# Padding the large tiles of a hybrid RG-LRU, attention and expert-choice block to 256-byte offsets, and other forms for its routing

## The chip, the cores and the metric

The kernel runs on one core of a Trainium2 chip. The metric is device time in microseconds of one execution. The kernel before takes 1211.78 us (median of 3 runs, 1211.24 to 1212.25).

## The reference, cut to what matters

One transformer-like block over 1024 tokens of width 1024, all in float32: a modulated norm, an input projection into five parts, a recurrent branch (a short convolution and two gated linear recurrences), a differential attention branch with 4 heads, an output projection, and a feed-forward part in which each of 16 experts chooses its 128 tokens.

```python
h = rms_norm(x, g_norm1) * (1.0 + scale1) + shift1
x_lru, z_lru, q, k, v = jnp.split(jnp.dot(h, w_in), SPLITS, axis=-1)
y_lru = (rg_lru(conv(x_lru), forward) + rg_lru(conv(x_lru), backward)) * gelu(z_lru)
y_att = diff_attention(q, k, v, ...)
x = x + gate1 * jnp.dot(concat([y_lru, y_att]), w_out)
h2 = rms_norm(x, g_norm2) * (1.0 + scale2) + shift2
aff = softmax(jnp.dot(h2, w_router))              # [1024, 16]
g, idx = top_k(aff.T, 128)                        # 128 tokens for each expert
xe = h2[idx]
y = (silu(xe @ w1[e]) * (xe @ w3[e])) @ w2[e] * g # for e in 16 experts, 1024 x 1024 each
x = x + gate2 * scatter_add(idx, y)
```

## The kernel before, in words

A float32 value is split into two float32r parts, hi (a copy, ScalarE) and lo (the rest, a subtraction on VectorE or GpSimd), and a product takes three matmuls: hi by hi, hi by lo, lo by hi. All of these go through the helper at L92; their tiles tell them apart. A matmul here has 512 columns of a moving operand against a 128x128 stationary operand, which a weight load brings in for each matmul.

The stages in order: the input stage with the first projections (tiles `pjx`, moving operand `hh`/`hl` of pool `hp`, stationary `w0h`/`w0l` of pool `ylp`); projections `pjq`, `pjk`, `pjz`, `pjv` (operands in pools `hp` and `strm`), with the recurrences beside them; attention (`sc`, `pw`, `pv`); the output projection `mix` in eight token tiles t, with the norm, the router's logits and their softmax for each t; the routing; and the experts.

The mix stage (L1010 to L1101) runs, for each t: split the activations (`yh`, `yl`, pool `xw`), 48 matmuls against `who`/`wlo`/`wos` (pools `wo1` and `qkp`), add `x` (L1027), square sums on ScalarE, an inverse square root by three Newton steps on VectorE (L1054 to L1062, operands of one column), the logits (`pl`, `pk`), the softmax (L1072 to L1078, in the SBUF tile `lg`), values below the smallest normal number set to zero and each of 16 columns repeated 8 times (`afd`, L1081), a copy to `affs` (L1083), a transpose `pq` and two copies of it, `aTh` (the upper halves, as bfloat16) and `aT`, which have 128 rows (expert e, digit j) and 1024 tokens. The last tile, t = 7, is cut in three column pieces (`mix`, `mix7b`, `mix7c`).

The routing (L1169 to L1220) finds each expert's 128th largest value by nine counts. A count (L1124 to L1131) compares 1024 tokens with a threshold per row on VectorE (`junk`, with the sum in `cnt`), turns the sum into 0 or 1 (`sat`), and adds the 8 digits of an expert by a matmul with `bone`; then the next threshold `thr` and its companion `cth` are made (L1134, L1180, and `stp` at L1182). The operands are one to seven columns wide. Meanwhile GpSimd splits `affs` in three bfloat16 parts (L1145 to L1149) and makes `wl` of the first three weight tiles. The chosen slots, the pick of indices for expert 0, its gather and some filler matmuls (`warm`) follow.

The experts: 24 weight tiles each (16 of w1 and w3, 8 of w2; 512 KB each), which the SP queue loads into a ring of 37 buffers from several pools; a load is issued when the buffer's last tile has been split. Each tile is split into `wh` (ScalarE, 3 buffers) and `wl` (VectorE, 3 buffers), both in pool `wo1`, and used as moving operand in 6 matmuls: 96 of `ab` (stationary `xeh`, `xel`, pool `moe`), then 48 of `y` (stationary `hth`, `htl`, pool `moe`). The tokens of the next expert are picked meanwhile: GpSimd makes the one-hot tiles `oh` (8 instructions, L1236), which start when the transposes `pf` have freed their buffer; 8 small matmuls `pi`, queued on TensorE between `y` of this expert and `ab` of the next, read them; a gather by GpSimd follows.

SBUF is laid out by pools: some stack up from the low end (`const`, `ylp`, `qkp` or `lru`, `wo1`, `late0`, `late`, `moe`), others down from the high end (`rawA`, `vp`, `hp`, `strm`, later `ap`, `xw`). Tiles begin at multiples of 32 bytes. With the sizes of the small tiles as they are, the start addresses modulo 256 are: 96 in `ylp`, `qkp`, `lru`, `wo1`, `late0` and `late`; 160 in `moe`; 224 in `rawA`, `vp`, `hp`, `strm` and the large tiles of `xw`; 32 in `ap`. A large tile has 4096 bytes per partition, and its parts used by one matmul are multiples of 512 bytes apart, so all matmuls of a kind have the same two residues.

The order of instructions on VectorE and TensorE is as written in the routing; in the mix stage and the experts a planner sets it, with `issue_after` as the only hints.

Of the kernel before, what the change touches and what calls it, by code (L numbers as in the profile page):

```python
# [18 lines left out]
P = 128  # L19
# [6 lines left out]
NE = 16  # L26
# [55 lines left out]
def tile_block(ctx: ExitStack, tc, x, cols, w_mod, b_mod, w_in, wa, wx, lam_qk, relT, w_out, g2, w_router,  # L82
# [17 lines left out]
    SY.dma_start(out=col, in_=cols)  # L100
    epsc = const.tile([P, 1], F32, name="epsc")
    V.memset(epsc, EPS)

# [7 lines left out]


    rawA = ctx.enter_context(tc.tile_pool(name="rawA", bufs=NRA, side="right"))
    vp = ctx.enter_context(tc.tile_pool(name="vp", bufs=1, side="right"))
# [66 lines left out]
    gqk = tbl.tile([P, 2], F32, name="gqk")  # L181
    go8 = const.tile([P, 1], F32, name="go8")
    jb = const.tile([P, 1], I32, name="jb")
    jf = const.tile([P, 7], F32, name="jf")
    relt = tbl.tile([NH, 32], F32, name="relt")
    A.dma_start(out=relt, in_=relT)
    nlam = const.tile([P, 1], F32, name="nlam")
    ls = const.tile([P, 2], F32, name="ls")
    lq = sm1.tile([P, 4, 64], F32, name="lq")
# [505 lines left out]
    s_sum = const.tile([P, NH, NT, 2], F32, name="s_sum")  # L695
    stat0 = const.tile([P, 1, 3], F32, name="stat0")
    scp, pt_, wts, pvs, ots = {}, {}, {}, {}, {}
# [85 lines left out]
    phw = ExitStack()  # L783
    psa = phw.enter_context(tc.tile_pool(name="psa", bufs=1, space=PSUM, reuse_waits="tile"))
    stat = ap.tile([P, NH * NT - 1, 3], F32, name="stat")

# [111 lines left out]
    with tc.manual_schedule(engines={mybir.EngineType.PE, mybir.EngineType.DVE, mybir.EngineType.Activation}):  # L898
        for g in range(NG + 2):
# [54 lines left out]
    xt_ = {nm: xw.tile(sh, F32, name=nm) for nm, sh in (  # L954
        ("sum4", [P, NE]), ("wr2", [P, KT, NE]), ("wrA", [P, KT, 32]), ("lg", [P, NT, NE]), ("hov", [P, 4]), ("hot", [P, 4]),
        ("hoy", [P, 4]), ("l4", [P, P]), ("afd", [P, P]))}
    xb_ = {nm: xw.tile([P, D], F32R if nm[0] == "y" else F32, tag=nm, bufs=1, name=nm + "_0") for nm in XO}
# [24 lines left out]
    rs2 = const.tile([P, NT], F32, name="rs2")  # L982
    lg = xt_["lg"]
    lmx = const.tile([P, 2 * NT], F32, name="lmx")
    aT = late0.tile([P, S], F32, tag="big", bufs=1, name="aT")
    lsc = late.tile([P, S], F32, tag="big", bufs=1, name="lsc")
    aTh = lsc[:, 0:512].bitcast(BF16)
    rstm = lsc[:, 512:640].bitcast(BF16).rearrange("p (a t) -> p a t", t=NT)
    rem = lsc[:, 640:768].rearrange("p (t e) -> p t e", e=NE)
# [16 lines left out]
    for t in range(NT):  # L1006
# [46 lines left out]
        if t == NT - 1:  # L1053
            V.tensor_tensor(out=ssq2[:, t, 0:1], in0=ssq2[:, t, 0:1], in1=ssq2[:, t, 1:2], op=ALU.add)  # L1054
        v, u, y = ssq2[:, t, 0:1], ssq2[:, t, len(cuts) - 2:len(cuts) - 1], rs2[:, t:t + 1]
        V.scalar_tensor_tensor(out=v, in0=v, scalar=EPS, in1=u, op0=ALU.add, op1=ALU.add)
        V.tensor_scalar(out=y.bitcast(I32), in0=v.bitcast(I32), scalar1=1, scalar2=None, op0=ALU.logical_shift_right)
        V.tensor_scalar(out=v, in0=v, scalar1=-0.5, scalar2=None, op0=ALU.mult)
        V.tensor_scalar(out=y.bitcast(I32), in0=y.bitcast(I32), scalar1=-1, scalar2=0x5F3759DF, op0=ALU.mult, op1=ALU.add)
        for _ in range(3):  # L1060
            V.scalar_tensor_tensor(out=u, in0=y, scalar=v, in1=y, op0=ALU.mult, op1=ALU.mult)
            V.scalar_tensor_tensor(out=y, in0=u, scalar=1.5, in1=y, op0=ALU.add, op1=ALU.mult)  # L1062
        pl = psa.tile([P, P], F32, tag="pv", bufs=1, name=f"pl{t}")
        for k in range(KT):
# [5 lines left out]
        mm(pl[:, 0:NE], l4, sum4, True, True)  # L1070
        lt = lg[:, t, :]
        V.scalar_tensor_tensor(out=lt, in0=pl[:, 0:NE], scalar=rs2[:, t:t + 1], in1=s2w, op0=ALU.mult, op1=ALU.add)  # L1072
# [4 lines left out]
        V.reciprocal(out=sm, in_=sm)  # L1077
        V.tensor_scalar(out=lt, in0=lt, scalar1=sm, scalar2=None, op0=ALU.mult)  # L1078
        afd = xt_["afd"]
        ltb = lt.unsqueeze(2).to_broadcast([P, NE, 8])  # L1080
        i_afd = V.scalar_tensor_tensor(out=afd.rearrange("p (e j) -> p e j", j=8), in0=ltb, scalar=TINY, in1=ltb,  # L1081
                                       op0=ALU.is_ge, op1=ALU.mult)
        i_aff = V.tensor_copy(affs[:, t, :], afd.rearrange("p (e j) -> p e j", j=8)[:, :, 0])  # L1083
        pq = psa.tile([P, P], F32, tag="pv", bufs=1, name=f"pq{t}")
        T.transpose(pq, afd, ident)
        act(aTh[:, sl], pq.bitcast(BF16)[:, 1::2])
        i_aT = act(aT[:, sl], pq)
        (A if t in OA else SY).dma_start(out=out[sl, :], in_=x1)
        if t < NT - 1:
# [21 lines left out]
    junk = moe.tile([P, S], BF16, tag="os", bufs=1, name="junk")  # L1111
    lo = const.tile([P, 1], I32, name="lo")
    thr = const.tile([P, 1], I32, name="thr")
    ni = const.tile([P, 1], I32, name="ni")
    cnt = const.tile([P, 1], F32, name="cnt")
    sat = const.tile([P, 1], BF16, name="sat")
    cth = const.tile([P, 1], F32, name="cth")
    pw8 = const.tile([P, 7], F32, name="pw8")
    stp = const.tile([P, 7], F32, name="stp")
    lof, thf = lo.bitcast(F32), thr.bitcast(F32)  # L1120
    for i in range(7):
        G_.memset(pw8[:, i:i + 1], 2.0 ** (-5 - 3 * i))

    def count(name, src, during=()):  # L1124
        first = V.tensor_scalar(out=junk, in0=src, scalar1=thf, scalar2=None, op0=ALU.is_ge, op1=ALU.add, accum_out=cnt)
        V.tensor_scalar(out=sat, in0=cnt, scalar1=float(CAP), scalar2=None, op0=ALU.is_ge)
        for f_ in during:
            f_()
        pn = pst.tile([P, 1], F32, tag="pn", bufs=2, name=name)
        mm(pn, bone, sat, True, True)  # L1130
        return pn, first  # L1131

    def axpy(o, a, b, c):
        return lambda: V.scalar_tensor_tensor(out=o, in0=a, scalar=b, in1=c, op0=ALU.mult, op1=ALU.add)  # L1134

    NR = 5
    rhs = late.tile([P, NT, NE, NR], BF16, name="rhs")
    tidx = late.tile([P, NT], F32, name="tidx")
    pidx = late.tile([P, 1], F32, name="pidx")
# [11 lines left out]
    G_.tensor_copy(selb, bone.rearrange("p (e j) -> p e j", j=8)[:, :, 0])  # L1151
    sts = const.tile([P, 1], F32, name="sts")
    idx = const.tile([P, NE], I32, name="idx")
# [14 lines left out]

    V.tensor_copy(thr, jb)  # L1169
    V.tensor_copy(cth, jf[:, 4:5])  # L1170
    with tc.manual_schedule(engines={mybir.EngineType.DVE, mybir.EngineType.PE}):
        during = []
        for i in range(3):
            pn, c_ = count(f"pb{i}", aTh, during)
            first = c_ if i == 0 else first
            s_ = float(1 << (27 - 3 * i))
            axpy(thr if i < 2 else lo, pn, s_, cth)()
            if i < 2:
                axpy(cth, pn, s_, cth)()
                during = [lambda i=i: V.tensor_tensor(out=cth, in0=cth, in1=jf[:, 5 + i:6 + i], op=ALU.add)]  # L1180
        V.tensor_scalar(out=ni, in0=lo, scalar1=0x7F800000, scalar2=None, op0=ALU.bitwise_and)
        V.tensor_tensor(out=stp, in0=pw8, in1=ni.bitcast(F32).to_broadcast([P, 7]), op=ALU.mult)  # L1182
        axpy(thf, jf[:, 0:1], stp[:, 0:1], lof)()
        during = [axpy(cth, jf[:, 1:2], stp[:, 0:1], lof)]
        for i in range(6):
            pn, _ = count(f"pv{i}", aTh if i == 0 else aT, during)
            axpy(thf, pn, stp[:, i:i + 1], cth)()
            during = [axpy(cth, jf[:, 2:3], stp[:, i:i + 1], thf) if i < 5 else axpy(cth, jf[:, 3:4], stp[:, 6:7], thf)]
        pth = pst.tile([P, NE, 1], F32, tag="pth", name="pth")
# [21 lines left out]

        m0, c0 = (const.tile([P, 2, 1, NT], BF16, name=nm) for nm in ("m0", "c0"))
        s0 = const.tile([P, 2, 1, NT], F32, name="s0")
        slot0 = const.tile([P, 1, NT], F32, name="slot0")
        slots(1, m0, c0, s0, slot0)
# [236 lines left out]
```

## Time and profile before

| | us |
|---|---|
| runs (median of 3) | 1211.78 |
| the profiled execution | 1212.75 |
| its span | 1210.7 |
| input, projections, recurrences | 0 to 312 |
| attention | to 480 |
| mix | to 593 |
| routing, up to expert 0's first matmuls | to 629 |
| 16 experts | to 1200 |

The 2.05 us between the span and the execution's time lie before and after the program's instructions. TensorE was busy for 93% of the span, VectorE for 80%. Of the page's 40 slices (30.3 us each) the 20th and the 21st (575 to 636 us) have TensorE busy for four and five tenths; from the 22nd on it is at nine or more up to the last. The chain of waits (what released what, back from the last instruction) is TensorE for 72% of the span, VectorE for 9%, DMA for 7% and GpSimd for 4%. In the rows below PE is TensorE, DVE VectorE, ACT ScalarE, POOL GpSimd, SP the queue that issues most loads.

### The profile page before, as it was taken

The page shows a single profiled execution, that of the slowest core. Times are in us where ns is not written, and L with a number is a line of the kernel's source. Part 1 is how long each engine was busy: PE and PEld are TensorE (multiplying, and loading weights), DVE is VectorE, ACT ScalarE, POOL GpSimd, SP SyncE. Part 2 cuts the span into 40 slices and gives each one's busy share as a digit, 9 for nine tenths or more (in the row PEclk, how much of TensorE's full clock was granted, in tenths as well). Part 3 has the DMA queues.
Part 4 walks back from the last instruction along what each step waited for, and adds up shares of the span by engine and source line. Part 5 has one row for each costly group of instructions (what it writes and reads, how often), then busy time and mean ns, then how long its engine had stood idle before and what let it go on. Part 6 is the DMA issues. An engine that isn't in the chain of part 4 may idle for free.

```text
span 1210.7 us, 17872 instructions
## 1 busy us (share of the span) xinstructions
PE 1131.7 (93%) x6319; PEld 938.4 (78%) x6320; DVE 963.9 (80%) x1248; ACT 790.8 (65%) x1038; POOL 486.2 (40%) x540
## 2 busy tenths in 40 slices
PE   6899999998699999999459999999999999999996
PEld 4699998888589899777337788888888888887885
DVE  6698566863399886544769999999999999999995
ACT  6547372492378787433318777777777777877774
POOL 4683321142276545333624334443323444332400
PEclk9999999999799999999769999999999999999998
DMA  9864726615753414435779999999999999999921
GB/s 313 235 206 161 245 69 218 217 36 92 205 122 110 126 36 154 155 127 209 263 269 324 352 368 379 377 393 383 381 383 382 370 380 395 383 383 382 380 59 17
DMA packets 147889, 303.81 MB, mean 251 GB/s; under 512 B 17997, under 2 KB 44749, under 8 KB 147797
## 3 DMA queue, kind: packets, MB, share of 16 engines
q1 hardware_dynamic: 134864, 279.46, 66.3%
q0 software_dynamic: 5488, 19.45, 6.2%
q10 hardware_dynamic: 7448, 3.77, 1.1%
q8 instruction: 49, 0.80, 0.3%
q14 instruction: 40, 0.32, 0.1%
HBM read 277.42 MB, written 25.22 MB: 250 GB/s over the span
## 4 chain that ended last, share of the span: by engine, by line
PE 72%; DVE 9%; DMA 7%; POOL 4%; issue 4%; ACT 2%; SPq 1%; POOLq 0%; DVEq 0%; ACTq 0%
PE ab L92 28%; PE y L92 13%; PE mix L92 5%; PE pjk L92 4%; PE pjz L92 3%; PE pv L92 3%; PE sc L92 3%; POOL wo L877 2%; PE pjv L92 2%; PE pjx L92 2%; PE pjq L92 2%; DVE macc L615 1%; DMA wr<-in_w_mod_dram 1%; PE pw L805 1%; PE pg L92 1%
## 5 line engine op out<-in xcount | busy, mean ns | idle before, releaser
L1236 POOL TENSOR_SCALAR oh<-iot,slot 128x128 bf16<-128x128 bf16 x120 | 147.6, 1245 | 259.8 <-PE pf L1336 259.8
L92 PE MATMUL ab<-wh,xeh 128*128 128x512 f32 x512 | 205.0, 401 | 0.0
L92 PE MATMUL ab<-wh,xel 128*128 128x512 f32 x512 | 202.4, 395 | 0.0
L92 PE MATMUL ab<-wl,xeh 128*128 128x512 f32 x512 | 161.0, 395 | 0.0
L92 PEld LDWEIGHTS ab<-wl,xeh 128*128 128x128 f32 x512 | 96.2, 188 | 23.2
L92 PEld LDWEIGHTS ab<-wh,xel 128*128 128x128 f32 x512 | 96.3, 188 | 22.1 <-DVE xel L1249 0.5
L92 PEld LDWEIGHTS ab<-wh,xeh 128*128 128x128 f32 x512 | 96.1, 188 | 22.2 <-ACT xeh L89 0.2
L128 DVE TENSOR_TENSOR wl<-w_0r,wh 128x1024 fp32r<-128x1024 f32 x79 | 96.8, 1226 | 13.2 <-ACT wh L89 12.5
L89 ACT ACTIVATE wh<-w_0r 128x1024 fp32r<-128x1024 f32 x81 | 86.1, 1063 | 28.0 <-PE ab L92 16.8
L128 DVE TENSOR_TENSOR wl<-w_3r,wh 128x1024 fp32r<-128x1024 f32 x79 | 96.7, 1225 | 9.4 <-ACT wh L89 8.2
L89 ACT ACTIVATE wh<-w_3r 128x1024 fp32r<-128x1024 f32 x79 | 83.9, 1062 | 25.7 <-PE ab L92 21.1
L89 ACT ACTIVATE wh<-w_1r 128x1024 fp32r<-128x1024 f32 x79 | 83.5, 1059 | 25.8 <-PE ab L92 20.0
L128 DVE TENSOR_TENSOR wl<-w_2r,wh 128x1024 fp32r<-128x1024 f32 x80 | 96.5, 1221 | 3.1 <-ACT wh L89 3.1
L89 ACT ACTIVATE wh<-w_2r 128x1024 fp32r<-128x1024 f32 x80 | 84.7, 1060 | 20.1 <-PE ab L92 19.6
L128 DVE TENSOR_TENSOR wl<-w_1r,wh 128x1024 fp32r<-128x1024 f32 x78 | 92.6, 1219 | 4.3 <-ACT wh L89 2.8
L760 DVE CUSTOM_DVE_ANT_0 p<-sc,bias 128x1024 f32<-128x1024 f32 x64 | 77.7, 1214 | 19.1 <-PE sc L92 19.1
L92 PE MATMUL y<-wh,htl 128*128 128x512 f32 x256 | 84.0, 400 | 0.0
L92 PE MATMUL y<-wh,hth 128*128 128x512 f32 x256 | 82.0, 400 | 0.0
L92 PE MATMUL y<-wl,hth 128*128 128x512 f32 x256 | 80.8, 396 | 0.0
L89 ACT ACTIVATE p<-p,stat 128x1024 f32<-128x1024 f32 x64 | 73.1, 1151 | 4.9 <-DVE stat L760 4.9
L92 PEld LDWEIGHTS pv<-v,wt 128*128 128x128 f32 x512 | 61.7, 192 | 2.4
L92 PE MATMUL pv<-v,wt 128*128 128x128 f32 x512 | 62.1, 275 | 0.0
(454 smaller groups left out, 2868.6 us busy)
## 6 DMA issues: line engine op xcount, KB each, us to landing
w_0r<-in_w_dram SPq DMA_DIRECT2D x81, 512.0 KB, 9.6
w_1r<-in_w_dram SPq DMA_DIRECT2D x79, 512.0 KB, 10.0
w_2r<-in_w_dram SPq DMA_DIRECT2D x78, 512.0 KB, 9.5
w_3r<-in_w_dram SPq DMA_DIRECT2D x77, 512.0 KB, 10.7
wr<-in_w_mod_dram SPq DMA_DIRECT2D x32, 512.0 KB, 4.4
wi<-in_w_in_dram SPq DMA_DIRECT2D x18, 512.0 KB, 4.3
w_5r<-in_w_dram SPq DMA_DIRECT2D x17, 512.0 KB, 6.5
wm<-in_w_mod_dram SPq DMA_DIRECT2D x32, 256.0 KB, 5.9
```

What stands on the lines that cost most here:

```text
L89: return A.activation(out=out, in_=in_, func=func, **kw)
L92: return T.matmul(out, lhsT=lhsT, rhs=rhs, start=start, stop=stop)
L128: return (eng or V).tensor_tensor(out=lo, in0=src, in1=hi.bitcast(F32), op=ALU.subtract)
L615: V.scalar_tensor_tensor(out=macc[i], in0=w, scalar=sc[:, k:k + 1], in1=macc[i], op0=ALU.mult, op1=ALU.add)
L760: V.tensor_tensor_reduce(out=p_, in0=scp[g, j], in1=prs[h][0][:, b0:b0 + S], op0=ALU.add, op1=ALU.min, scale=1.0, scalar=3.0e38, accum_out ...
L805: T.transpose(pw[:, b * P:(b + 1) * P], pt_[g, 0][:, kt * P:(kt + 1) * P], ident)
L877: G_.tensor_tensor(out=r[:, qs], in0=r[:, qs], in1=gate1[:, qs], op=ALU.mult)
L1236: G_.tensor_scalar(out=oh[:, t, :], in0=iot, scalar1=slot[:, e, t:t + 1], scalar2=None, op0=ALU.is_equal)
```

## The change

It does four things. First, padding: twenty small tiles of `const` become parts of one tile `misc` (78 columns), unused tiles (`rpad`, `appad0`, `appad1`, `xwpad`) and a longer `tidx` are added, so that the sums of small tiles come to multiples of 256 bytes: by the same arithmetic as above, the large tiles of `ylp`, `qkp`, `lru`, `wo1`, `late0`, `late`, `moe`, `rawA`, `vp`, `hp`, `strm`, `ap` and `xw` then all start at residue 0. (`xT` of the input stage goes from residue 0 to 160.) Second, VectorE instructions with two SBUF tensors of one or seven columns become `tensor_scalar` with one tensor and pointer scalars. Third, the softmax of the logits stays in the PSUM tile of `pk`, and the copy to `affs` goes from VectorE to ScalarE. Fourth, the first count is taken in two parts: 896 tokens within the mix stage, behind the second add of t = 7, and the last 128 in its place.

```diff
+RPAD = 56
...
-    epsc = const.tile([P, 1], F32, name="epsc")
+    misc = const.tile([P, 78], F32, name="misc")
+    epsc, go8, nlam, ls, jb, jf = (misc[:, a:b] for a, b in ((0, 1), (1, 2), (2, 3), (3, 5), (5, 6), (6, 13)))
+    lo, thr, ni, cnt, sat, cth = (misc[:, a:a + 1] for a in range(13, 19))
+    pw8, stp, sts, stat0, slot0, s0, m0, c0 = (misc[:, a:b] for a, b in ((19, 26), (26, 33), (33, 34), (34, 37), (37, 45),
+                                                                         (45, 61), (61, 69), (69, 77)))
+    cnt7 = misc[:, 77:78]
...
+    rpad = ctx.enter_context(tc.tile_pool(name="rpad", bufs=1, side="right"))
+    rpad.tile([P, RPAD], F32, name="rpad")
     rawA = ctx.enter_context(tc.tile_pool(name="rawA", bufs=NRA, side="right"))
...
+    ap.tile([P, 32], F32, name="appad0")
     stat = ap.tile([P, NH * NT - 1, 3], F32, name="stat")
...
+    ap.tile([P, 16], F32, name="appad1")
     pah.close()
...
-        ("sum4", [P, NE]), ("wr2", [P, KT, NE]), ("wrA", [P, KT, 32]), ("lg", [P, NT, NE]), ("hov", [P, 4]), ("hot", [P, 4]),
-        ("hoy", [P, 4]), ("l4", [P, P]), ("afd", [P, P]))}
+        ("sum4", [P, NE]), ("wr2", [P, KT, NE]), ("wrA", [P, KT, 32]), ("lgm", [P, NT, NE]), ("hov", [P, 4]), ("hot", [P, 4]),
+        ("hoy", [P, 4]), ("l4", [P, P]), ("afd", [P, P]), ("xwpad", [P, 24]))}
...
+    SE = (NT - 1) * P
...
+            if n == 1 and t == NT - 1:
+                with tc.issue_after(add.ins):
+                    V.tensor_scalar(out=x_big("yh0", NT).bitcast(BF16)[:, 0:SE], in0=aTh[:, 0:SE], scalar1=jb.bitcast(F32),
+                                    scalar2=None, op0=ALU.is_ge, op1=ALU.add, accum_out=cnt7)
...
-            V.tensor_tensor(out=ssq2[:, t, 0:1], in0=ssq2[:, t, 0:1], in1=ssq2[:, t, 1:2], op=ALU.add)
+            V.tensor_scalar(out=ssq2[:, t, 0:1], in0=ssq2[:, t, 0:1], scalar1=ssq2[:, t, 1:2], scalar2=None, op0=ALU.add)
...
-        V.scalar_tensor_tensor(out=v, in0=v, scalar=EPS, in1=u, op0=ALU.add, op1=ALU.add)
+        V.tensor_scalar(out=v, in0=v, scalar1=EPS, scalar2=u, op0=ALU.add, op1=ALU.add)
...
-            V.scalar_tensor_tensor(out=u, in0=y, scalar=v, in1=y, op0=ALU.mult, op1=ALU.mult)
-            V.scalar_tensor_tensor(out=y, in0=u, scalar=1.5, in1=y, op0=ALU.add, op1=ALU.mult)
+            V.tensor_scalar(out=u, in0=y, scalar1=v, scalar2=y, op0=ALU.mult, op1=ALU.mult)
+            V.tensor_scalar(out=y, in0=u, scalar1=1.5, scalar2=y, op0=ALU.add, op1=ALU.mult)
...
-        lt = lg[:, t, :]
+        lt = pl[:, 32:32 + NE]
...
-        V.tensor_scalar(out=lt, in0=lt, scalar1=sm, scalar2=None, op0=ALU.mult)
+        msk_ = lgm[:, t, :]
+        V.tensor_scalar(out=msk_, in0=lt, scalar1=sm, scalar2=TINY, op0=ALU.mult, op1=ALU.is_ge)
         afd = xt_["afd"]
-        ltb = lt.unsqueeze(2).to_broadcast([P, NE, 8])
-        i_afd = V.scalar_tensor_tensor(out=afd.rearrange("p (e j) -> p e j", j=8), in0=ltb, scalar=TINY, in1=ltb,
-                                       op0=ALU.is_ge, op1=ALU.mult)
-        i_aff = V.tensor_copy(affs[:, t, :], afd.rearrange("p (e j) -> p e j", j=8)[:, :, 0])
+        V.scalar_tensor_tensor(out=afd.rearrange("p (e j) -> p e j", j=8), in0=lt.unsqueeze(2).to_broadcast([P, NE, 8]), scalar=sm,
+                               in1=msk_.unsqueeze(2).to_broadcast([P, NE, 8]), op0=ALU.mult, op1=ALU.mult)
...
         i_aT = act(aT[:, sl], pq)
+        act(affs[:, t, :], afd.rearrange("p (e j) -> p e j", j=8)[:, :, 0])
...
-    def count(name, src, during=()):
-        first = V.tensor_scalar(out=junk, in0=src, scalar1=thf, scalar2=None, op0=ALU.is_ge, op1=ALU.add, accum_out=cnt)
-        V.tensor_scalar(out=sat, in0=cnt, scalar1=float(CAP), scalar2=None, op0=ALU.is_ge)
+    def count(name, src, during=(), part=False):
+        o, i, th = (junk[:, SE:], src[:, SE:], jb.bitcast(F32)) if part else (junk, src, thf)
+        first = V.tensor_scalar(out=o, in0=i, scalar1=th, scalar2=None, op0=ALU.is_ge, op1=ALU.add, accum_out=cnt)
+        if part:
+            V.tensor_scalar(out=sat, in0=cnt, scalar1=cnt7, scalar2=float(CAP), op0=ALU.add, op1=ALU.is_ge)
+        else:
+            V.tensor_scalar(out=sat, in0=cnt, scalar1=float(CAP), scalar2=None, op0=ALU.is_ge)
...
+    def step(o, a, b, c):
+        return lambda: V.tensor_scalar(out=o, in0=a, scalar1=b, scalar2=c, op0=ALU.mult, op1=ALU.add)
...
-    tidx = late.tile([P, NT], F32, name="tidx")
+    tidx = late.tile([P, 56], F32, name="tidx")[:, 0:NT]
...
-    V.tensor_copy(thr, jb)
...
-            pn, c_ = count(f"pb{i}", aTh, during)
+            pn, c_ = count(f"pb{i}", aTh, during, i == 0)
...
-                during = [lambda i=i: V.tensor_tensor(out=cth, in0=cth, in1=jf[:, 5 + i:6 + i], op=ALU.add)]
+                during = [lambda i=i: V.tensor_scalar(out=cth, in0=cth, scalar1=jf[:, 5 + i:6 + i], scalar2=None,
+                                                      op0=ALU.add)]
...
-        V.tensor_tensor(out=stp, in0=pw8, in1=ni.bitcast(F32).to_broadcast([P, 7]), op=ALU.mult)
-        axpy(thf, jf[:, 0:1], stp[:, 0:1], lof)()
-        during = [axpy(cth, jf[:, 1:2], stp[:, 0:1], lof)]
+        V.tensor_scalar(out=stp, in0=pw8, scalar1=ni.bitcast(F32), scalar2=None, op0=ALU.mult)
+        step(thf, jf[:, 0:1], stp[:, 0:1], lof)()
+        during = [step(cth, jf[:, 1:2], stp[:, 0:1], lof)]
...
-            during = [axpy(cth, jf[:, 2:3], stp[:, i:i + 1], thf) if i < 5 else axpy(cth, jf[:, 3:4], stp[:, 6:7], thf)]
+            during = [step(cth, jf[:, 2:3], stp[:, i:i + 1], thf) if i < 5 else step(cth, jf[:, 3:4], stp[:, 6:7], thf)]
```

## Rows read from the trace of the kernel before

**Rows 1.** Windows, one expert: us, PE, PEld, DVE, ACT, POOL, clock, DMA share, GB/s.

```profile
695.70:731.40 35.70, 35.70 (x170) 28.69 (x169) 33.64 (x35) 28.19 (x31) 13.95 (x11) 1.00 1.04 371
```

**Rows 2.** The chain in order of time, one expert's turn: start us, us, what.

```profile
702.81 12.70 PE ab L92 x54
...
730.58 7.70 PE y L92 x33
...
738.47 12.71 PE ab L92 x54
```

**Rows 3.** The chain in order of time, projections and mix.

```profile
175.39 10.91 PE pjz L92 x48
...
511.57 5.36 PE mix L92 x23
```

**Rows 4.** Timeline of POOL, experts: start us, us, engine line op tiles [idle before].

```profile
654.94 11.96 POOL L1236 TENSOR_SCALAR oh<-iot,slot 128x128 bf16<-128x128 bf16 x8 [13.61 <-PE pf L1336]
...
727.76 10.07 POOL L1236 TENSOR_SCALAR oh<-iot,slot 128x128 bf16<-128x128 bf16 x8 [18.91 <-PE pf L1336]
```

**Rows 5.** Timeline of PE, 737 to 739 us.

```profile
738.12 0.35 PE L92 MATMUL pi<-rhs,oh 128*128 128x5 bf16 x8
```

**Rows 6.** Waits of the SP queue, 640 to 1150 us: us in total, times, longest.

```profile
SPq L1287 <- DVE wl L128: 177.1, 171, 3.5
```

**Rows 7.** Timeline of DVE, 593 to 606 us.

```profile
593.38 1.28 DVE L1125 TENSOR_SCALAR_CACHE_REDUCE junk<-lsc,thr 128x1024 bf16<-128x1024 bf16 x1 [0.67 <-ACT lsc L89]
...
595.11 0.16 DVE L1134 SCALAR_TENSOR_TENSOR thr<-pb,cth 128x1 int32<-128x1 f32 x1 [0.26 <-PE pb L92]
...
596.69 0.16 DVE L1126 TENSOR_SCALAR sat<-cnt 128x1 bf16<-128x1 f32 x1
596.76 1.78 DVE L1180 TENSOR_TENSOR cth<-cth,jf 128x1 f32<-128x1 f32 x1
598.64 0.16 DVE L1134 SCALAR_TENSOR_TENSOR thr<-pb,cth 128x1 int32<-128x1 f32 x1
...
600.29 1.99 DVE L1180 TENSOR_TENSOR cth<-cth,jf 128x1 f32<-128x1 f32 x1
...
602.77 1.82 DVE L1182 TENSOR_TENSOR stp<-pw,ni 128x7 f32<-128x7 f32 x1
```

**Rows 8.** Timeline of POOL, 593 to 606 us.

```profile
596.17 2.35 POOL L128 TENSOR_TENSOR wl<-w_0r,wh 128x1024 fp32r<-128x1024 f32 x1
598.46 0.54 POOL L1147 CAST rhs<-lsc 128x128 bf16<-128x128 f32 x1
...
602.23 2.34 POOL L128 TENSOR_TENSOR wl<-w_1r,wh 128x1024 fp32r<-128x1024 f32 x1
```

**Rows 9.** DVE groups by shape, whole span: busy us, mean ns, idle before.

```profile
L794 DVE TENSOR_SCALAR stat<-stat,nlam,s_sum 128x1 f32<-128x1 f32 x32 | 8.6, 269 | 0.0
...
L1078 DVE TENSOR_SCALAR lg<-lg,lmx 128x16 f32<-128x16 f32 x8 | 3.4, 425 | 0.2
...
L1193 DVE TENSOR_SCALAR sts<-cnt,stp 128x1 f32<-128x1 f32 x1 | 0.2, 212 | 0.0
```

**Rows 10.** Timeline of DVE, 579 to 591 us.

```profile
581.71 1.36 DVE L1081 SCALAR_TENSOR_TENSOR afd<-lg 128x128 f32<-128x128 f32 x1
583.10 2.24 DVE L1083 COPY affs<-afd 128x16 f32<-128x16 f32 x1
585.26 0.41 DVE L1027 TENSOR_TENSOR xr<-mix7b,xr 128x256 f32<-128x256 f32 x1
...
587.69 0.42 DVE L1027 TENSOR_TENSOR xr<-mix7c,xr 128x256 f32<-128x256 f32 x1 [0.64 <-PE mix7c L92]
...
589.41 0.22 DVE L1061 SCALAR_TENSOR_TENSOR ssq<-rs,ssq 128x1 f32<-128x1 f32 x1
589.66 0.16 DVE L1062 SCALAR_TENSOR_TENSOR rs<-ssq,rs 128x1 f32<-128x1 f32 x1
```

**Rows 11.** Waits of PE, 470 to 593 us: us in total, times, longest.

```profile
PE pq L1085 <- DVE afd L1081: 4.5, 6, 2.3
```

More of the change, by code (lines that the diff above doesn't have):

```diff
@@ L100, in tile_block @@
     SY.dma_start(out=col, in_=cols)
-    epsc = const.tile([P, 1], F32, name="epsc")
+    misc = const.tile([P, 78], F32, name="misc")
[4 more added lines that the diff above has]
+    cnt7 = misc[:, 77:78]
+    jb, lo, thr, ni = (t_.bitcast(I32) for t_ in (jb, lo, thr, ni))
+    sat = sat.bitcast(BF16)[:, 0:1]
+    stat0 = stat0.unsqueeze(1)
+    slot0 = slot0.rearrange("p (a t) -> p a t", a=1)
+    s0 = s0.rearrange("p (a n t) -> p a n t", a=2, n=1)
+    m0, c0 = (t_.bitcast(BF16).rearrange("p (a n t) -> p a n t", a=2, n=1) for t_ in (m0, c0))
     V.memset(epsc, EPS)
@@ L181, in tile_block @@
     gqk = tbl.tile([P, 2], F32, name="gqk")
-    go8 = const.tile([P, 1], F32, name="go8")
-    jb = const.tile([P, 1], I32, name="jb")
-    jf = const.tile([P, 7], F32, name="jf")
     relt = tbl.tile([NH, 32], F32, name="relt")
     A.dma_start(out=relt, in_=relT)
-    nlam = const.tile([P, 1], F32, name="nlam")
-    ls = const.tile([P, 2], F32, name="ls")
     lq = sm1.tile([P, 4, 64], F32, name="lq")
@@ L695, in tile_block @@
     s_sum = const.tile([P, NH, NT, 2], F32, name="s_sum")
-    stat0 = const.tile([P, 1, 3], F32, name="stat0")
     scp, pt_, wts, pvs, ots = {}, {}, {}, {}, {}
@@ L982, in tile_block @@
     rs2 = const.tile([P, NT], F32, name="rs2")
-    lg = xt_["lg"]
+    lgm = xt_["lgm"]
     lmx = const.tile([P, 2 * NT], F32, name="lmx")
@@ L1111, in tile_block @@
     junk = moe.tile([P, S], BF16, tag="os", bufs=1, name="junk")
[L1112 to L1119, printed above, removed]
     lof, thf = lo.bitcast(F32), thr.bitcast(F32)
@@ L1151, in tile_block @@
     G_.tensor_copy(selb, bone.rearrange("p (e j) -> p e j", j=8)[:, :, 0])
-    sts = const.tile([P, 1], F32, name="sts")
     idx = const.tile([P, NE], I32, name="idx")
@@ L1210, in slots @@
             V.tensor_tensor(out=o, in0=s_[:, 0], in1=s_[:, 1], op=ALU.add)
-        m0, c0 = (const.tile([P, 2, 1, NT], BF16, name=nm) for nm in ("m0", "c0"))
-        s0 = const.tile([P, 2, 1, NT], F32, name="s0")
-        slot0 = const.tile([P, 1, NT], F32, name="slot0")
         slots(1, m0, c0, s0, slot0)
```

## The prediction

> **What bounds the kernel now.** I read three views. First the windows by stage. In one expert's turn TensorE is busy for all of its 35.70 us at a granted clock of 1.00, VectorE for 33.64 us, and the DMA share is 1.04 [rows 1]. So the experts, the largest stage, go at the pace of TensorE unless VectorE or the loads are close behind. The chain in order of time says the same: nothing but TensorE, and the next turn starts 35.66 us later (702.81 to 738.47) [rows 2].
>
> Second, that chain gives the pace of a matmul: 33 of `y` in 7.70 us are 233.3 ns each; 54 of `ab` in 12.70 us are 235.2 ns with the small transitions [rows 2]. The same shape elsewhere: 48 of `pjz` in 10.91 us are 227.3 ns, 23 of `mix` in 5.36 us are 233.0 ns [rows 3]. What differs is where the operands lie. Moving and stationary operand start modulo 256 at 224 and 224 for `pjz`, at 96 and 160 for `ab` and `y`, at 96 and 224 for `mix`. Only the pair with equal residues is at 227.
>
> Third, VectorE's timeline of the routing, where one engine after the other works and TensorE hardly does: three two-tensor instructions of one to seven columns take 1.78, 1.99 and 1.82 us [rows 7], and each ends when a GpSimd instruction ends (596.17 + 2.35 = 598.52, and 602.23 + 2.34 = 604.57; a third such pair lies between) [rows 7, 8]. A `tensor_scalar` of one column, `sat` at 596.69, took 0.16 us in the middle of the same GpSimd instruction. So it is the second tensor that waits for GpSimd.
>
> **The change part by part.**
>
> *Padding, experts.* After it every large tile starts at residue 0, so all pairs are equal, as `pjz` is. A matmul then costs 227.3 instead of 233.3 ns. There are 16 x 144 = 2304 of them: 13.8 us. Expert 1's pick already makes TensorE wait (GpSimd's 11.96 us there against 10.07 us later, [rows 4]), so the 48 `y` of expert 0 gain nothing (0.3 us): -13.5 us. The bounds: 0, if the residues are not the cause, and -16.1 us, at 7 ns a matmul, should an offset of 0 do better than equal residues; no settled run of matmuls in the rows is slower than the present one, which excludes a loss. I take the value of `pjz`, the only row with equal residues.
>
> By the Trainium skill, "SBUF — State Buffer", Who interferes with whom, TensorE has separate read ports for moving operand and weight load and waits for no one: then this term would be 0, which is a rival below. The rows do not agree that all pairs cost the same, but none shows why.
>
> What is late next? VectorE needs 33.64 us a turn and would have 34.8. The loads: SP's issue waits mostly for VectorE to free a ring buffer [rows 6], and with 37 buffers at 1.49 us (35.70 / 24) a load is asked for about 55 us ahead. If the DMA could go no faster than now, it would fall behind by 0.9 us a turn, 13 us in all, and the lead covers that: cost 0. The pick of the next expert: GpSimd's `oh` ends at 727.76 + 10.07 = 737.83, `pi` starts at 738.12 and needs its last tile some 0.2 us later [rows 4, 5]. That slack of nearly 0.5 us shrinks by 48 x 6 ns = 0.3 us. GpSimd's instructions fall into the gaps of VectorE's, which TensorE paces, so they shrink too: cost 0, a rival below.
>
> *Routing.* First count: 128 columns instead of 1024. Of the 1.28 us [rows 7] some 0.21 is fixed (the one-column form, [rows 9]); 0.21 + 1.07 / 8 = 0.35 remains, -0.93, and `sat` gets a pointer, 0.21 for 0.16: -0.88 us together. The 896 columns before it cost 0.21 + 0.94 + 0.08 (the read of the sum) = 1.2 us in VectorE's queue; they wait for the copy `aTh` of t = 6 and for the buffer `yh0`, and behind them stand the sum of L1054 and the add at 587.69. VectorE is free from 585.67 to 587.69 but for L1054 [rows 10], so `mix7c` hides them; without that cover they cost up to 1.2 us.
>
> `cth`, twice: from `sat` to `thr` is 0.42 us when nothing blocks (0.16 and a wait of 0.26 for TensorE, at 595.11); blocked it is 598.64 - 596.69 = 1.95, and 2.17 the second time [rows 7]. With one column and one tensor, 0.21 us, it fits in TensorE's wait: -1.53 and -1.75 us. `stp` has seven columns. Its bounds are 0.2 us (one-column form) and 2.35 us (a whole GpSimd split); moved 4.2 us earlier it starts near 598.6, in the cast of 0.54 us at 598.46 [rows 8]. I take 0.5: -1.3 us, with -1.6 and +0.5 as ends. `thr` and the last `cth` get two pointers, 0.269 for 0.22 [rows 9]: +0.1. Sum -5.4 us, ends -5.7 and -3.6.
>
> On `stp`, the Trainium skill, "SBUF — State Buffer", Who interferes with whom, says that a Vector instruction with one SBUF tensor leaves GpSimd's port alone unless it runs in a two-port mode, which `tensor_scalar` may. The row for L1078, 16 columns, agrees: 425 ns on average though it takes 230 when GpSimd rests. One-column rows show no such wait.
>
> *Mix.* The Newton steps of t = 7 lie on the path and run unblocked there: three times 0.269 for 0.22 and 0.212 for 0.16 [rows 9, 10], and one more pointer: +0.3 us. For t = 6, `afd` took 1.36 us behind a GpSimd instruction and the copy of `affs` 2.24 us, which held the add at 585.26 [rows 10]. With the logits in PSUM neither has two SBUF tensors, and `affs` is ScalarE's, behind `aT`, where GpSimd asks for it only after its subtraction of 2.3 us. `afd` becomes some 0.35 us: -1.0, ends 0 and -1.3. No row shows the softmax on PSUM operands; the nearest is the add at 585.26 from PSUM, 0.41 us for 256 columns, so an instruction of 16 columns lies between 0.15 and 0.41, against some 0.2 now: 0, ends -0.2 and +0.4 at t = 7. Holding the one PSUM buffer `pv` for the softmax delays no one: its next user, `pq`, waits for `afd` anyway. For the other tiles TensorE's waits for `afd` are 4.5 - 2.3 = 2.2 us [rows 11], and 336 matmuls gain 5.7 ns each, 1.9 us; the two trade against each other, so I take -2.0 together, ends 0 and -4.1.
>
> *Elsewhere.* The first projections, `sc` and `pv`, with unequal or barely settled pairs: -0.3 us, ends +0.3 and -2. Loads into aligned tiles may start work sooner; the chain's loads before 312 us are short, 0.
>
> **Sum.** -13.5 - 5.4 + 0.3 - 1.0 - 2.0 - 0.3 = -21.9 us. From the profiled execution (1212.75 us: the span of 1210.7 and 2.05 around it) this is 1190.9 us; the median of 1211.78 is 0.97 below that execution, so 1190 us.
>
> **The rivals.**
>
> *The residues do nothing.* For it: only one stage has equal residues, and other engines work differently there. Against it: `mix` and `y`, in stages with quite different company, are both at 233. Then the expert and half of the mix term fall away: -5.4 + 0.3 - 1.0 - 0.5 = -6.6, 1205 us.
>
> *VectorE becomes the bound.* It has 2.06 us to spare in a turn [rows 1]. If its waits for ScalarE keep half of the gain from coming, 6.8 us less: 1197 us. Against it: those waits come from buffers that TensorE frees, so they shorten with it.
>
> *The pick becomes the bound, and the kernel slower.* The place is `pi` between two experts. If GpSimd, squeezed by a denser VectorE, needs the 11.96 us of expert 2 instead of 10.07 [rows 4], then beyond the slack of 0.5 - 0.3 = 0.2 us TensorE waits 1.7 us in each of 14 turns, 24 us: 1214 us. From 11.8 us a pick on it cancels the whole gain. Against it: 13 of 14 turns look like the one at 727.76.
>
> *The loads become the bound* would need the lead to run out, 55 us against 13; with `pjz`'s pace lost it gives the 1205 us of the first rival, and is counted there.
>
> **How the numbers follow.** The forecast 70%, its own range 1185 to 1196 us by the ends of its terms; no effect of the residues 14%; VectorE 8%; the pick 5%; 3% for something unseen, of either sign, such as a wait that the shared tile `misc` brings. The range 1185 to 1207 us takes in the first three and leaves out the pick. About 0.2% (2.4 us) is what can be told from no change: faster 0.93, the same 0.02, slower 0.05.
>
> **What would show it.** In a turn of an expert: 33 `y` in 7.50 us instead of 7.70, the next turn 34.8 us later, VectorE at 97%. `pi` without waits. In the routing: `cth` at 0.2 us behind `sat`, a first count of 0.35 us, `stp` below 0.6. At t = 7: Newton steps of 0.27 and 0.21, the count of 896 columns between the second and the third add. The prediction is wrong if `y` stays at 233 ns a matmul with both operands at residue 0, or if TensorE shows waits for `oh` in most turns.

## The result, and the profile after

The changed kernel takes 1189.48 us (median of 4 runs, 1187.79 to 1191.91); the kernel before took 1211.51 us beside it. The ratio is 0.9819, 95% interval 0.9801 to 0.9837, or 22 us less. The profiled execution took 1189.59 us, its span is 1187.8 us. TensorE is busy for 94% of it and VectorE for 80%.

The stages, from the first start of each kind of instruction in the timelines (us):

| from .. to | before | after | difference | forecast |
|---|---|---|---|---|
| start .. first `mix` matmul | 473.97 | 473.82 | -0.15 | -0.3 |
| .. last `mix7c` matmul | 113.41 | 107.98 | -5.43 | -3.0 |
| .. first count | 6.00 | 6.30 | +0.30 | +0.3 |
| .. fourth count (first `pv`) | 11.50 | 6.01 | -5.49 | -5.5 |
| .. `pi` of expert 0 | 15.84 | 16.10 | +0.26 | +0.1 |
| .. first `ab` | 8.80 | 7.75 | -1.05 | 0 |
| .. last `y` | 570.92 | 559.74 | -11.18 | -13.5 |

One turn of an expert in the windows of the kernel after (columns as in [rows 1]), and the same turn in its chain:

```profile
689.82:724.77 34.95, 34.95 (x175) 28.62 (x172) 33.52 (x35) 28.18 (x31) 13.80 (x10) 1.00 1.04 381
```

```profile
689.82 0.20 PE pi L93 x8
690.03 12.37 PE ab L93 x54
702.39 0.50 PE pf L1346 x4
...
717.26 7.51 PE y L93 x33
...
724.97 12.40 PE ab L93 x54
```

The turn is 34.94 us (690.03 to 724.97) against 35.66 [rows 2]. 33 `y` at 227.6 ns stand where 233.3 were, 54 `ab` in 12.37 us where there were 12.70. VectorE is at 96% of the turn. The group of transposes `pf` takes 0.50 us where it took 0.44. From the chain before:

```profile
715.51 0.44 PE pf L1336 x4
```

Two tiles of mix in the chain of the kernel after, and the waits of TensorE from 470 to 588 us (us in total, times, longest):

```profile
510.27 5.49 PE mix L93 x24
...
523.61 5.49 PE mix L93 x24
```

```profile
PE pq L1099 <- DVE afd L1096: 2.7, 1, 2.7
PE pl L93 <- ACT x1T L90: 0.5, 1, 0.5
PE pk L93 <- ACT l L90: 0.4, 1, 0.4
```

A tile takes 13.34 us (510.27 to 523.61) where it took 14.16: 511.57 [rows 3] to the next such group in the chain before,

```profile
525.73 5.38 PE mix L92 x23
```

Of the six waits for `afd` in [rows 11] one is left, that of t = 7 behind the last matmul.

VectorE and GpSimd in the routing of the kernel after:

```profile
588.10 0.35 DVE L1133 TENSOR_SCALAR_CACHE_REDUCE junk<-lsc,misc 128x128 bf16<-128x128 bf16 x1 [0.73 <-ACT lsc L90]
...
592.60 0.20 DVE L1192 TENSOR_SCALAR misc<-misc 128x1 f32<-128x1 f32 x1
592.94 0.16 DVE L1145 SCALAR_TENSOR_TENSOR misc<-pb,misc 128x1 int32<-128x1 f32 x1
...
593.32 0.44 DVE L1195 TENSOR_SCALAR misc<-misc 128x7 f32<-128x7 f32 x1
```

```profile
591.38 2.34 POOL L142 TENSOR_TENSOR wl<-w_0r,wh 128x1024 fp32r<-128x1024 f32 x1
593.69 0.47 POOL L1162 TENSOR_TENSOR lsc<-lsc,rhs 128x128 f32<-128x128 f32 x1
```

The second `cth` (592.60) takes 0.20 us in the middle of GpSimd's `wl`; `stp` (593.32) ends at 593.76, as that `wl` does (593.72). In [rows 7] they took 1.99 and 1.82 us.

### The profile page after: what moved, and what is told of

It reads as the page before. It is cut to its first block, busy times and chain, and to the rows that moved or that the text cites. A ratio compares the mean times of both kernels' runs of the same rounds, so it can differ in the third digit from the quotient of the medians.

```text
span 1187.8 us, 17864 instructions
## 1 busy us (share of the span) xinstructions
PE 1115.3 (94%) x6319; PEld 935.9 (79%) x6320; DVE 955.2 (80%) x1241; ACT 791.6 (67%) x1046; POOL 484.1 (41%) x540
## 4 chain that ended last, share of the span: by engine, by line
PE 73%; DVE 7%; DMA 6%; POOL 6%; issue 5%; ACT 2%; SPq 0%; POOLq 0%; ACTq 0%; DVEq 0%
PE ab L93 28%; PE y L93 13%; PE mix L93 7%; PE pjk L93 3%; PE pjz L93 3%; PE pv L93 3%; PE sc L93 3%; POOL wo L886 2%; PE pjv L93 2%; DMA wr<-in_w_mod_dram 2%; PE pw L814 1%; PE pjx L93 1%; PE pf L1346 1%; PE pg L93 1%; DVE macc L624 1%
## 5 line engine op out<-in xcount | busy, mean ns | idle before, releaser
L93 PE MATMUL ab<-wh,xeh 128*128 128x512 f32 x512 | 202.0, 395 | 0.2 <-ACT xeh L90 0.2
L93 PE MATMUL ab<-wh,xel 128*128 128x512 f32 x512 | 199.7, 390 | 0.1
L93 PE MATMUL ab<-wl,xeh 128*128 128x512 f32 x512 | 157.7, 389 | 0.0
```

The costliest lines, as they stand in the source:

```text
L93: return T.matmul(out, lhsT=lhsT, rhs=rhs, start=start, stop=stop)
```

## The experiments

The times of whole runs of one kernel scatter by 2 us and more (by 9 in one of them), and the start of mix alone lies between 469.88 and 474.59 us in the profiles of these kernels, though most leave what is ahead of it alone. So besides the runs I read the stages: mix (first `mix` matmul to last), routing (first count to fourth), experts (first `ab` to last `y`). Where an expectation speaks of the time from the first count to the sixth (11.5 us before, 6.0 after), it is the time to the fourth count of the table that is meant; the sixth starts 15.57 us behind the first before and 10.15 after.

**The two halves apart.** The first kernel has the padding and the instructions of before, the second the new instructions and the residues of before:

```diff
 # pad_only: before, and
+    misc = const.tile([P, 78], F32, name="misc")   # with the small tiles in it
+    rpad.tile([P, RPAD], F32, name="rpad")
...
 # forms_only: after, and
-    misc = const.tile([P, 78], F32, name="misc")
+    misc = const.tile([P, 102], F32, name="misc")
-    rpad.tile([P, RPAD], F32, name="rpad")
...
-    tidx = late.tile([P, 56], F32, name="tidx")[:, 0:NT]
+    tidx = late.tile([P, 72], F32, name="tidx")[:, 0:NT]
```

> The kernel before with the padding alone: the shared tile misc and the unused tiles, so that all large tiles start at a multiple of 256 bytes; every instruction has the form it had before. Theory 1 (a matmul is slower when its two operands start at different residues modulo 256): y at 227 ns a matmul instead of 233, a turn of an expert 34.95 us instead of 35.66, the experts 11 us shorter; mix also at 228 ns, but there VectorE's chain holds much of it back, 1 to 2 us; the routing as before (cth near 1.8 and 2.0 us). Time 1198 to 1200 us. Rival (the residues do nothing, the new forms did all of it): y at 233 ns, a turn of 35.66 us, 1211.5 us.

> The changed kernel with the padding taken out, so that the large tiles stand at the residues of the kernel before (96, 160, 224, 32); the new instruction forms, the softmax in PSUM and the early first count stay. Theory 1: experts as before (y 233 ns, a turn 35.66 us), the routing as in the changed kernel (from the first count to the sixth 6.0 us instead of 11.5), the mix stage 3 to 4 us shorter. Time 1200 to 1202 us, so that the two halves add up to the whole of 22 us. Rival (residues do nothing): 1189.5 us, with y at 227 ns here too.

Measured: padding alone 1197.02 us, ratio 0.9866 (0.9847 to 0.9885); forms alone 1202.91 us, ratio 0.9931 (0.9906 to 0.9957). Experts 560.06 and 570.91 us (before 570.92, after 559.74); routing 11.48 and 5.85; mix 112.76 and 108.80. The whole times give 15.1 and 9.2 us, together 2 us more than the change. So the experts' gain is the padding's, the routing's is the forms', and the forms hold nearly all of mix; the rival in which the residues do nothing has fallen. In the chain of waits, first padding alone, then forms alone:

```profile
727.67 7.53 PE y L93 x33
735.40 12.40 PE ab L93 x54
```

```profile
720.19 7.70 PE y L93 x33
728.09 12.71 PE ab L93 x54
```

**What about the residues counts.** All large tiles at 96; then the stationary ones of experts and mix alone at 64; then the moving ones alone at 64; all are the kernel after with other sizes of the three paddings:

```diff
 # all96: left pools + 96, right pools + 96
+    misc = const.tile([P, 102], ...)      RPAD = 32
 # stat64: moe, and the right pools with xw, + 64
+    RPAD = 40      tidx = late.tile([P, 72], ...)
 # mov64: the left pools below moe + 64
+    misc = const.tile([P, 94], ...)       tidx = late.tile([P, 40], ...)
```

> The changed kernel with every large tile moved by the same 96 bytes: all residues are 96, none is 0. Theory 1 (only the difference of the two operands counts): the time of the changed kernel, 1189.5 us within 2, y at 227 ns, a turn 34.95 us. Rival (each operand has to start at a multiple of 256 bytes): y at 233 ns, a turn near 35.7 us, 1200 us or more.

> The changed kernel with the stationary operands alone moved by 64 bytes in the experts and in the mix stage (pools moe, xw and the others on the high side at 64), the moving ones still at 0. Theory 1: y at 233 ns as with 96 against 160 before, mix near 233, a turn 35.65 us, 1201 us. Rival (it is enough that the moving operand starts at a multiple of 256): y at 227 ns and 1189.5 us.

> The changed kernel with the moving operands alone moved by 64 bytes in the experts and in the mix stage (pools ylp, qkp, wo1, late0 and late at 64), the stationary ones at 0. Theory 1 (the difference counts, in either direction): y at 233 ns, a turn of an expert 35.65 us, 1202 us, as with the stationary ones moved. Rival (only the stationary operand has to be aligned): y at 227 ns, 34.95 us a turn, 1189.5 us.

Measured: 1190.28 us, ratio 0.9809 (0.9792 to 0.9827); 1202.59, ratio 0.9914 (0.9897 to 0.9932); 1192.11, ratio 0.9831 (0.9803 to 0.9859). The chains, in this order:

```profile
717.91 7.51 PE y L93 x33
```

```profile
720.37 7.70 PE y L93 x33
```

```profile
716.88 7.58 PE y L93 x33
```

Equal residues that are not 0 are as fast as 0 (227.6 ns), and 64 bytes on the stationary side alone bring 233.3 back, with experts of 570.89 us: the pair counts, as the prediction had it, and not the multiple of 256. But the other direction broke my rule that any difference costs the same: with the moving operand at 64, `y` is at 229.7 ns and the experts at 562.63 us, a quarter of the loss. So two more kernels gave each stationary operand a residue of its own, with the moving ones at 0:

```diff
+        if kind in ("yo", "hth", "htl", "g2"):
+            moe_pad(kind)                 # an unused tile ahead of it in moe
...
 # curve1: hth 32, htl 64, xeh 128, xel 192, mix 192 (RPAD = 8)
 # curve2: hth 96, htl 160, xeh and xel 224, mix 224 (no rpad)
```

> The changed kernel with the moving operands of the experts and of mix at 0 and each stationary one at a residue of its own: hth 32, htl 64, xeh 128, xel 192, the activations of mix 192. So far: stationary minus moving, modulo 256, of 0 gave 227 ns a matmul, of 64 gave 233.4, of 192 (moving at 64, stationary at 0) only 229.5, so theory 1 holds in this form: the pace depends on the signed difference. Theory 1a: it falls in a ramp from 64 to 256, so 32 or 64 next to 32 gives 233 to 235 (y), 128 next to 192 gives 230 to 231 (ab), a turn 35.3 us. Theory 1b: any stationary operand that is not at 0 costs the full 6 ns when the moving one is at 0: 233 for all, a turn 35.65 us.

> The same with hth at 96, htl at 160, xeh and xel at 224, the activations of mix at 224, all moving operands at 0. Theory 1a (ramp): ab at 228 to 229 ns with a difference of 224, y at 231 to 232 with 96 and 160; a turn 35.15 us. Theory 1b: 233 for all, 35.65 us.

Measured, one run each: 1200.67 and 1202.89 us, turns of 35.61 and 35.61 us, experts 570.32 and 570.34:

```profile
719.17 7.68 PE y L93 x33
```

```profile
721.56 7.68 PE y L93 x33
```

The ramp (theory 1a) has fallen: 96, 160 and 224 cost as much as 64. Theory 1b fits these two, but mix in the first of them (192) took 107.98 us, as with equal residues, and 108.79 in the second (224); 64 gave 108.96, and the moving operand at 64 (which is 192 as well, signed) 108.12. So 0 is fast, 192 lies near it in these three cases, and the other differences that were tried, from 32 to 224, cost all or nearly all of it. Why, and whether a matmul's own weight load or that of the next one is what meets the moving operand, stays open. The `ab` of curve1 start 230 to 236 ns apart, and not by their residue alone: of the six matmuls of a weight tile the first, third and fifth take 230.2 to 231.7 ns on average, the second, fourth and sixth 235.2 to 236.0, though the fifth and the sixth both have `xeh` (128). Nor was it tried whether 256 is the period: no kernel was made to put two operands 256 bytes apart.

**The routing: form or neighbour.** The kernel after with two tensors again in `cth`, `stp` and the steps, and the same with the three `wl` of GpSimd made by ScalarE as plain copies (it leaves out their subtraction, so its output is not the block's):

```diff
 # two_tensor
-   V.tensor_scalar(out=cth, in0=cth, scalar1=jf[:, 5 + i:6 + i], scalar2=None, op0=ALU.add)
+   V.tensor_tensor(out=cth, in0=cth, in1=jf[:, 5 + i:6 + i], op=ALU.add)
...
 # two_tensor_nogp, besides
-            parts[i] = wparts(i, G_)
+            parts[i] = wparts(i, A)
...
+        if eng is A:
+            return act(lo, src)
```

> The changed kernel with the routing's small instructions back in the forms with two tensors (cth twice, stp, the steps of thr and cth); the early first count and the padding stay. Theory (a second SBUF tensor waits for a GpSimd instruction that is running): cth and stp take 1 to 2.3 us where GpSimd splits wl or rhs, and from the first count to the sixth it is 9 to 11 us instead of 6.0: 1193 to 1195 us. Rival (the form itself costs, wherever it stands): 0.16 to 0.22 us each as in quiet places, no longer than now, 1189 us.

> The same forms with two tensors, but the wl of the first three weight tiles is made by ScalarE, as a plain copy (the subtraction is left out), so that GpSimd has only its short work on rhs in the routing. Theory (it is GpSimd's long subtraction that holds the second tensor): cth and stp at 0.2 us once rhs is done, at most 0.6 beside it; from the first count to the sixth 6.0 to 6.8 us; 1189 to 1190 us. Rival (the two-tensor form is slow in this place for another reason, such as the tile misc that all small values share): 9 us or more here too.

Measured: 1192.59 us, ratio 0.9846 (0.9811 to 0.988), routing 8.83 us; and 1186.22, ratio 0.9781 (0.9752 to 0.9809), routing 5.86. The first is a little under what I expected, since the first `cth` fell beside short GpSimd instructions (0.42 us). VectorE of the two-tensor kernel, then its GpSimd, then VectorE without GpSimd's `wl`:

```profile
590.07 0.97 DVE L1192 TENSOR_TENSOR misc<-misc 128x1 f32<-128x1 f32 x1
...
591.86 2.32 DVE L1145 SCALAR_TENSOR_TENSOR misc<-misc 128x1 f32<-128x1 f32 x1
```

```profile
588.67 2.35 POOL L142 TENSOR_TENSOR wl<-w_0r,wh 128x1024 fp32r<-128x1024 f32 x1
...
591.82 2.34 POOL L142 TENSOR_TENSOR wl<-w_0r,wh 128x1024 fp32r<-128x1024 f32 x1
```

```profile
588.76 0.15 DVE L1194 TENSOR_TENSOR misc<-misc 128x1 f32<-128x1 f32 x1
...
589.48 0.17 DVE L1196 TENSOR_TENSOR misc<-misc 128x7 f32<-128x7 f32 x1
589.68 0.22 DVE L1147 SCALAR_TENSOR_TENSOR misc<-misc 128x1 f32<-128x1 f32 x1
```

Each blocked instruction ends when `wl` does (591.04 and 591.02, 594.18 and 594.16), and without a `wl` beside them they take 0.15 to 0.22 us. So the second tensor costs what the neighbour makes it wait; neither the form by itself nor the shared tile `misc` is slow. (The last kernel's profile is 3.1 us shorter than that of the kernel after. All of it is ahead of mix, 469.88 against 473.82 us, where the two do not differ; its routing gains 0.15 us, and its stretch from `pi` to the first `ab` is 1.05 us longer.)

**The first count whole.**

```diff
-            if n == 1 and t == NT - 1:
-                with tc.issue_after(add.ins):
-                    V.tensor_scalar(out=..., in0=aTh[:, 0:SE], ..., accum_out=cnt7)
...
-        o, i, th = (junk[:, SE:], src[:, SE:], jb.bitcast(F32)) if part else (junk, src, thf)
+        o, i, th = (junk, src, jb.bitcast(F32)) if part else (junk, src, thf)
```

> The changed kernel with the first count whole again: 1024 tokens in its place, none counted within the mix stage. The first count takes 1.28 us instead of 0.35 and the sixth starts 0.9 us later; if the early count of 896 is hidden in the mix stage, as I hold, that is the whole difference: 1190.4 us. Rival: the early count delays the sums behind it in VectorE's queue, and the last add to first count is 0.3 to 1 us shorter without it, so that nothing is lost: 1189.5 us.

Measured: 1191.66 us, ratio 0.9839 (0.9792 to 0.9886), too wide to tell 0.9 from 3. From the last matmul of mix to the first count it is 6.31 us, against 6.30, so the early count is hidden, and that rival falls. But the fourth count came 3.1 us later and not 0.9. VectorE and GpSimd show why:

```profile
594.09 2.68 DVE L1191 TENSOR_SCALAR misc<-misc 128x7 f32<-128x7 f32 x1
```

```profile
594.10 0.54 POOL L1159 CAST rhs<-lsc 128x128 bf16<-128x128 f32 x1
594.40 2.34 POOL L142 TENSOR_TENSOR wl<-w_0r,wh 128x1024 fp32r<-128x1024 f32 x1
```

`stp` has one tensor now and still ends with the next `wl` (596.77 and 596.74); it is longer than that `wl`, since it began beside the cast ahead of it. In the kernel after it met only the last 0.44 us of the `wl` before. The short first count thus saves its 0.9 us and, by luck of place, 2.2 us of `stp`.

**Which half of mix.** The softmax back in SBUF, with the copy to `affs` on VectorE; and the Newton steps back in two tensors:

```diff
 # softmax_sbuf
-        lt = pl[:, 32:32 + NE]
+        lt = lgm[:, t, :]
...
-        act(affs[:, t, :], afd.rearrange("p (e j) -> p e j", j=8)[:, :, 0])
+        V.tensor_copy(affs[:, t, :], afd.rearrange("p (e j) -> p e j", j=8)[:, :, 0])
 # newton_stt
-            V.tensor_scalar(out=u, in0=y, scalar1=v, scalar2=y, op0=ALU.mult, op1=ALU.mult)
+            V.scalar_tensor_tensor(out=u, in0=y, scalar=v, in1=y, op0=ALU.mult, op1=ALU.mult)
```

> The changed kernel with the softmax of the logits back in an SBUF tile and the copy to affs back on VectorE; the Newton steps stay in the one-tensor form. In the mix stage a token tile took 14.16 us before and 13.34 after, though the padding alone changed nothing there. If it is the end of the softmax (afd, affs) that held TensorE: 14 us a tile again, and the last add 4 to 5 us later, 1193 to 1195 us. If it is the Newton steps: no more than 1 us later, most of it at t = 6, where afd and the copy stand behind GpSimd; 1190 us.

> The changed kernel with the Newton steps and the sums ahead of them (L1069 to L1077) back in the forms with two tensors; the softmax stays in PSUM. From the first mix matmul to the last it was 113.4 us before, 108.0 after; with the softmax alone put back 110.0. If the two parts add up: 2.5 to 3 us longer than now, near 110.7, and some 0.3 us less from the last matmul of mix to the first count (the new forms cost that much at t = 7); 1191 to 1192 us. If the softmax is all that held TensorE and the rest was t = 6: under 0.5 us, 1189.5 us.

Measured: 1190.64 us, ratio 0.9818 (0.979 to 0.9847), mix 109.95; and 1191.64, ratio 0.9839 (0.9811 to 0.9866), mix 110.13. Each costs 2.0 to 2.2 us in mix, where I had expected either one half or the other to hold most of it, then 2.5 to 3 for the Newton steps. By whole times no difference of this size can be told; in mix the two together are 4.1 of the 4.8 that the forms give (112.76 with the padding alone, 107.98). TensorE's waits for `afd` from 474 to 593 us, which hold the 2.6 or 2.7 us of t = 7 in each kernel: softmax, then Newton, then the kernel after:

```profile
PE pq L1099 <- DVE afd L1096: 3.6, 2, 2.6
```

```profile
PE pq L1099 <- DVE afd L1096: 3.5, 4, 2.6
```

```profile
PE pq L1099 <- DVE afd L1096: 2.7, 1, 2.7
```

The old softmax brings back one wait (the step of t = 6, 1.0 us), the old Newton steps three, of 0.3 us each by this view; from start to start the matmul ahead of `pq` takes 677 ns there instead of some 235.

## Why the prediction was right

The forecast of 1190 us came out at 1189.5, and the mechanisms were the ones named. That the sum is so close is partly luck: the experts gave 2.3 us less than forecast, mix up to its last matmul 2.4 us more, and 1.05 us at the gather had not been foreseen. By its steps:

- *Experts, -13.5; -11.2 came.* The pace was right: 54 `ab` saved 6.1 ns each, 33 `y` 5.8. An expert gave 0.70 us on average (11.18 / 16) instead of 0.86. Of the rest 0.12 is the two groups `pf`, which take 0.50 instead of 0.44 us each. They wait for VectorE's product `sa`, by the waits of the weight loads in the experts, first before (700 to 1160 us), then after (690 to 1140 us):

```profile
PEld pf L1336 <- DVE sa L1333: 4.7, 26, 0.2
```

```profile
PEld pf L1346 <- DVE sa L1343: 6.8, 26, 0.3
```

  The nine `y` between the transposes gave 1.4 ns each (2.10 to 2.09 us), another 0.04. So the rival in which VectorE becomes the bound was there in small: 2 of its 6.8 us, by these waits.
- *The rivals.* The matmuls `pi` show no wait, and `oh` takes 9.96 us in a settled turn (714.47). The weight loads of `pi` do wait for `oh` in most turns, which the prediction named as a sign that it is wrong; but they did so before the change too, and not for less time. From the views of the weight loads, before and after (the windows of `sa` above):

```profile
PEld L92 <- POOL oh L1236: 3.6, 13, 0.3
```

```profile
PEld L93 <- POOL oh L1246: 3.1, 12, 0.3
```

  In both kernels `pi` takes 0.20 us of the chain, so these waits cost nothing there; the pick stayed behind TensorE. The DMA share is 1.04 as before, and no wait for a load is on the chain of a turn.
- *Routing, -5.4; -5.23 came.* From the timelines: first count with `sat` -0.87 (forecast -0.88), `cth` -1.54 and -1.76 (-1.53, -1.75), `stp` -1.37 (-1.3), `thr` behind it +0.05, then +0.26 for the two pointers of the later steps (+0.1 in all), 0.035 us in each of six counts and more behind them. `stp` met its value in another place than I put it, in the tail of a `wl`; that it came near the value is luck, as the whole first count shows: its 2.68 us would have been a loss of 0.9 on [rows 7], beyond the upper bound of +0.5, which took one whole `wl` as the most it could wait.
- *Mix at t = 7, +0.3: measured +0.30.* The count of 896 stands between the second and the third add, as forecast.
- *Mix up to the last matmul, -3.0; -5.4 came.* This is the mis-sized term; it stands at the end of its bounds, -5.4. The step that failed is "the two trade against each other". From start to start TensorE lost 0.22, 0.45, 0.48, 0.49 and 0.48 us ahead of `pq` in five tiles and 0.99 at t = 6, 3.1 us in all, where [rows 11] without t = 7 show 2.2: a wait counts from the modelled end of a matmul. With the shorter chain of VectorE all of this went, and the padding came on top: it is worth 0.65 us of mix without the new forms (113.41 to 112.76) and 0.82 with them (108.80 to 107.98). The two add up and do not trade. But the padding's part was mis-sized too: the prediction gave it 1.9 us, 5.7 ns for each of 336 matmuls, and with the padding alone the `mix` whose starts lie 215 to 245 ns apart (278 of them) go from 232.2 to 229.5 ns on average, 2.7 ns each. So the waits were worth more and the padding less, and that the sum meets the bound is luck. Of the 4.8 us of the forms 3.55 lie ahead of `pq`: its seven gaps from start to start in tiles 0 to 6 add up to 4.94 us with the padding alone and to 1.39 after. Most of the rest is right behind `pq` (0.4), between the matmuls of `pk` (0.4) and ahead of the transposes `ph` (0.5).
- *Elsewhere, -0.3.* From `pi` to the first `ab` 1.05 us went that no step foresaw. At the first transposes of the gathered tokens the granted clock was 0.51 before (627.35 to 629.52) and 1.00 after (616.61 to 617.95):

```profile
627.35:629.52 2.17, 2.17 (x10) 1.74 (x8) 0.00 (x0) 0.60 (x1) 2.17 (x4) 0.51 0.87 259
```

```profile
616.61:617.95 1.34, 1.09 (x9) 0.85 (x8) 0.00 (x0) 0.65 (x2) 1.34 (x4) 1.00 1.04 205
```

  I do not count it as a gain of the change: the fourteen profiles fall into two groups, 8.76 to 8.81 us (six, among them two_tensor_nogp, with all residues 0) and 7.58 to 7.96 us (eight, among them stat64). In the filler matmuls ahead of the transposes the granted clock is 0.50, the lower of its two levels (1.2 GHz), in all six; in all eight it rises there already, to 0.55 to 0.64 on average, and is at the upper one (1.00, 2.4 GHz) in the transposes. What makes it rise earlier or later was not tried.

By the Trainium skill, "SBUF — State Buffer", Who interferes with whom, TensorE's two read ports are independent and it never waits on anyone. The runs differ: with 64 bytes between the same two operands a `y` takes 233.3 instead of 227.6 ns, and the measurement decides. The same section says that a VectorE instruction with two SBUF inputs contends with a GpSimd instruction that reads SBUF, and that whoever has the shared ports first keeps them for the whole instruction; 2.32 us for a step that takes 0.22 without `wl` agrees.

## What to carry to other kernels

Where long runs of matmuls set the time, compare the start addresses of moving and stationary operand modulo 256 and bring them to the same residue: here it was worth 2.4% of a matmul and nearly 1% of the kernel, for unused bytes. A small VectorE instruction with two tensors beside a busy GpSimd has no price of its own: ask what GpSimd runs at that moment, and take the second tensor away, which was enough here for one column and not for seven, or move the instruction. Where a stall and the pace of what stalls are both mended, add the two, and take the stall from start to start rather than from a list of waits.

## What the runs showed of the hardware that was not expected

- The residues count in a signed way: stationary minus moving of 64 costs 5.7 ns a matmul, moving minus stationary of 64 only 2.1 (229.7 against 227.6).
- A `tensor_scalar` of seven columns waits for GpSimd (2.68 us) while one of a single column in the middle of the same kind of `wl` takes 0.20 us.
- The clock at the gather is one of two cases with 1.05 us between them, by whether the clock rises ahead of the first transposes or later, in profiles that differ by nothing else there that I could name.
